# First FFN stage: shift and scale from ScalarE scalings and a VectorE tree, 1/rms applied ahead, a look-ahead of two chunks, four classical pairs

## The chip, the core and the metric

The kernel runs on one core of one Trainium2 chip, in one launch, for a batch of one sequence of 512 tokens, model width 1024, hidden width 2816. The metric is the device time of that launch in microseconds. Five engines work side by side, each through its own instructions in order: TensorE (PE in the profile; its weight loads are PEld), VectorE (DVE), ScalarE (ACT), GpSimd (POOL) and SyncE (SP), which issues most of the DMA transfers. POOL issues the others, those that accumulate into on-chip memory and the stores.

## The reference

One decoder layer with three sub-layers, each with a norm that is scaled and shifted by columns computed from the condition `c`:

```python
def modulate(x, w, shift, scale):
    return rms_norm(x, w) * (1 + scale[:, None, :]) + shift[:, None, :]

def swiglu(h, w13, w2):
    gu = jnp.einsum('bsd,df->bsf', h, w13)
    g, u = jnp.split(gu, 2, axis=-1)
    return jnp.einsum('bsf,fd->bsd', jax.nn.silu(g) * u, w2)

c_act = jax.nn.silu(c)
mod = (jnp.einsum('bd,dn->bn', c_act, w_ada[l]) + b_ada[l]).reshape(b, N_SUB, 3, D_MODEL)
h = modulate(x, norm_w[l, 0], mod[:, 0, 0], mod[:, 0, 1])
x = x + 0.5 * mod[:, 0, 2][:, None, :] * swiglu(h, ffn_w13[l, 0], ffn_w2[l, 0])
h = modulate(x, norm_w[l, 1], mod[:, 1, 0], mod[:, 1, 1])
x = x + mod[:, 1, 2][:, None, :] * hybrid_mixer(h, ...)
h = modulate(x, norm_w[l, 2], mod[:, 2, 0], mod[:, 2, 1])
x = x + 0.5 * mod[:, 2, 2][:, None, :] * swiglu(h, ffn_w13[l, 1], ffn_w2[l, 1])
```

`hybrid_mixer` is latent attention beside a short gated convolution. All is float32. The work at issue lies in the first sub-layer: `mod[:, 0, 0]` and `mod[:, 0, 1]` (shift and scale), the norm, `h`, and the first products with `ffn_w13`.

## The kernel before, in words

**Layout.** x lies transposed, features on the 128 partitions, in KD = 8 chunks of 128 features by T = 512 tokens (two tiles x_in of four chunks each). Each float32 product is done as three matmuls on split operands (`mm3`, lines 132 to 135): high by high, low activation by high weight, high by low weight. A split (`split_to`, line 110) is a cast to the high part on ACT (line 111) and a subtract on DVE (line 112). A matmul is 128x128 by 256 columns.

**Shift and scale.** For chunk j a block of 1 MB of `w_ada` (tile ada, loaded by `ada01_load`, line 146) holds, for each of eight parts k of the condition, 128 shift and 128 scale columns. `ada_first` (200 to 207) multiplies it with `c_act` by 16 matmuls that have one moving column each (line 206), into ps, and `ada_finish` adds the bias on DVE into the columns of the tile mod (lines 186 and 188).

**The norm.** `Norm.add` squares a chunk on ACT (261) and sums it over the features: in sub-layer 0 by matmuls with a column of ones on PE (266, four per chunk), elsewhere by adding chunks on DVE (273) and four matmuls at the end (280). `rstd` (275) makes the power -1/2 on POOL, `spread` (287) turns it into rb, 1/rms along the tokens in all partitions (a matmul into PSUM, line 295). `chunk` (298) makes h of one chunk: x times g times rb on DVE (309), plus shift with the cast to the high part on ACT (310), the low part on DVE (311), and x plus shift on ACT, kept for later sums (314).

**The first FFN.** The hidden width is 22 tiles of 128. The first stage walks over the eight chunks and multiplies each with weights wfh, wfl of the first two hidden tiles (tiles pf_0 to pf_3: a gate and an up half for each, 24 matmuls per chunk); for chunk k it first issues, in `first_chunk` (758), the load of ada for chunk k+2, `ada_first` of chunk k+1, and then `chunk` of k. The remaining tiles come in jobs that `run` (453) works off. `pair_job` (520) computes a gate and up pair by a Strassen-Winograd scheme: seven products of 12 matmuls, with sums of h (T, made by `sums`, 316) and sums of weights: four loads and one more on SP (529) into sa and sb, two accumulating transfers on POOL (530, 531), and DVE sums (540, 543). `down_job` (586) multiplies the results a with the down weights d. The first down phase follows hidden tile 5, and takes 288 matmuls.

**Who sets the order.** A framework puts the instructions of each engine in an order of its own, from the program's order and its own estimates; each engine then runs strictly in that order. Blocks of 1 MB (17 buffers) hold x, ada, h, T and the raw weights: a load into one waits until its former user is done. In the first stage all eight PSUM banks are in use. SP's loads take eight lanes in turn, each waiting for the earlier one on its lane.

**Two further places.** `rope_tables` (709) makes the tables for the mixer on DVE and ACT, with eight operations on POOL (746); it is called behind the first stage. The norm of the mixer is taken in two halves of the tokens; `next(n1.steps)` (780) issues the `rstd` of the second half, whose matmuls are line 280, ahead of the mixer's latent products (800).

## Time and profile before

| | us |
|---|---|
| time, median of 3 runs (1147.9 to 1148.43) | 1147.91 |
| the profiled execution, its own time | 1150.7 |
| its span, first to last instruction | 1148.9 |
| its mean granted TensorE clock | 0.975 of full |

The span is cut into 40 equal slices of 28.7 us; a digit gives the busy share in tenths, PEclk the clock that was granted.

```profile
PE   8999799999999998999999999999999999999998
DVE  1228776984589757776747667747998468734873
ACT  3125434553355425455433433335764255524540
POOL 0000212201220011211100000001200221022001
PEclk9958899999999999999999999999999999999999
```

The rows are read from left to right: the first stage of the first FFN lies in slices 2 to 4, the mixer begins near slice 16. In the groups that the prediction shows, a row gives line, engine, operation, output and inputs by name, shapes, count, busy time, mean duration in ns, and the idle time ahead with what ended it. In lists of single rows the first two numbers are start and duration in us.

### The profile page before, as it was taken

What the parts mean: (1) busy time and instruction counts of PE and PEld (TensorE: products, weight loads), DVE (VectorE), ACT (ScalarE), POOL (GpSimd) and SP (SyncE); (2) the same over time, 40 slices, a digit from 0 to 9 for tenths busy, and PEclk for the clock granted to TensorE, in tenths of its full rate; (3) what the DMA queues carried; (4) which work ended last, traced back from release to release, by engine and by line L of the source; (5) the groups of instructions that cost most, each with busy time, mean ns of one, the idle gap of its engine ahead of it and who ended that gap; (6) DMA issues with size and microseconds to landing.
All of it is one profiled execution on the core that took longest, in us unless ns stands there. A gap on an engine that the chain in (4) does not pass through costs nothing.

```text
span 1148.9 us, 20412 instructions
## 1 busy us (share of the span) xinstructions
PE 1113.3 (97%) x8126; PEld 1051.3 (92%) x8126; DVE 772.8 (67%) x1312; ACT 494.1 (43%) x823; POOL 141.5 (12%) x173
## 2 busy tenths in 40 slices
PE   8999799999999998999999999999999999999998
PEld 7999799999999998888887777879999999999997
DVE  1228776984589757776747667747998468734873
ACT  3125434553355425455433433335764255524540
POOL 0000212201220011211100000001200221022001
PEclk9958899999999999999999999999999999999999
DMA  9342688957994643321135466854875985568452
GB/s 364 95 119 80 205 262 253 243 186 197 223 267 123 227 144 101 101 70 56 61 113 187 135 236 220 272 167 112 209 205 178 260 229 148 175 142 186 114 189 97
DMA packets 83984, 199.68 MB, mean 174 GB/s; under 512 B 9777, under 2 KB 12721, under 8 KB 80817
## 3 DMA queue, kind: packets, MB, share of 16 engines
q1 hardware_dynamic: 67408, 164.82, 43.2%
q0 software_dynamic: 16480, 33.56, 15.1%
q8 instruction: 63, 1.03, 0.4%
q14 instruction: 33, 0.26, 0.1%
HBM read 180.52 MB, written 17.83 MB: 173 GB/s over the span
## 4 chain that ended last, share of the span: by engine, by line
PE 71%; DMA 9%; issue 9%; DVE 7%; POOL 2%; ACT 1%; SPq 0%; POOLq 0%; DVEq 0%; ACTq 0%
PE g L133 5%; PE g L135 5%; PE g L134 5%; PE d L134 5%; PE d L133 5%; PE d L135 5%; PE u L133 4%; PE u L134 4%; PE u L135 4%; PE ps L206 3%; DMA sa<-in_w13a_dram 3%; PE pf L133 2%; PE pf L134 2%; PE pf L135 2%; PE p_gate L133 1%
## 5 line engine op out<-in xcount | busy, mean ns | idle before, releaser
L134 PE MATMUL d<-a,d_h 128*128 128x256 f32 x616 | 172.1, 279 | 0.0
L133 PE MATMUL d<-a,d_h 128*128 128x256 f32 x616 | 171.8, 279 | 0.0
L135 PE MATMUL d<-a,d_l 128*128 128x256 f32 x616 | 171.6, 279 | 0.0
L133 PE MATMUL u<-T,w_h 128*128 128x256 f32 x480 | 135.3, 282 | 2.5 <-ACT s L560 2.5
L134 PE MATMUL u<-T,w_h 128*128 128x256 f32 x480 | 134.7, 281 | 0.3 <-DVE T L112 0.3
L135 PE MATMUL u<-T,w_l 128*128 128x256 f32 x480 | 134.6, 280 | 0.0
L111 ACT CAST w_h<-sa 128x1024 fp32r<-128x1024 f32 x80 | 83.7, 1049 | 86.9 <-issue 52.6
L112 DVE TENSOR_TENSOR w_l<-sa,w_h 128x1024 fp32r<-128x1024 f32 x80 | 97.8, 1224 | 30.6 <-ACT w_h L111 16.6
L134 PEld LDWEIGHTS d<-a,d_h 128*128 128x128 f32 x616 | 115.9, 188 | 0.4 <-DVE a L112 0.3
L135 PEld LDWEIGHTS d<-a,d_l 128*128 128x128 f32 x616 | 116.2, 189 | 0.0
L133 PEld LDWEIGHTS d<-a,d_h 128*128 128x128 f32 x616 | 116.0, 189 | 0.2 <-ACT a L111 0.2
L133 PE MATMUL g<-h,w_h 128*128 128x256 f32 x320 | 90.1, 282 | 6.3 <-ACT s L565 6.2
L133 PEld LDWEIGHTS u<-T,w_h 128*128 128x128 f32 x480 | 91.1, 190 | 3.4 <-ACT s L560 3.4
L135 PEld LDWEIGHTS u<-T,w_l 128*128 128x128 f32 x480 | 91.7, 191 | 0.0
L134 PEld LDWEIGHTS u<-T,w_h 128*128 128x128 f32 x480 | 90.8, 189 | 0.5 <-DVE T L112 0.5
L134 PE MATMUL g<-h,w_h 128*128 128x256 f32 x320 | 89.9, 281 | 0.0
L135 PE MATMUL g<-h,w_l 128*128 128x256 f32 x320 | 89.9, 281 | 0.0
L133 PEld LDWEIGHTS g<-h,w_h 128*128 128x128 f32 x320 | 60.8, 190 | 6.7 <-ACT s L565 6.4
L111 ACT CAST d_h<-wdd 128x1024 fp32r<-128x1024 f32 (+1 forms) x42 | 40.8, 977 | 58.3 <-issue 33.6
L135 PEld LDWEIGHTS g<-h,w_l 128*128 128x128 f32 x320 | 61.3, 191 | 0.0
L112 DVE TENSOR_TENSOR d_l<-wdd,d_h 128x1024 fp32r<-128x1024 f32 (+1 forms) x42 | 47.6, 1133 | 19.9 <-ACT d_h L111 13.4
L112 DVE TENSOR_TENSOR w_l<-sb,w_h 128x1024 fp32r<-128x1024 f32 x40 | 48.8, 1221 | 17.7 <-PE g L134 15.5
(347 smaller groups left out, 3144.5 us busy)
## 6 DMA issues: line engine op xcount, KB each, us to landing
ada<-in_ada_dram SPq DMA_DIRECT2D x24, 1024.0 KB, 6.9
sa<-in_w13a_dram SPq DMA_DIRECT2D x80, 256.0 KB, 5.1
sa<-in_w13b_dram SPq DMA_DIRECT2D x80, 256.0 KB, 5.2
wdd<-in_w_dram SPq DMA_DIRECT2D x32, 512.0 KB, 4.5
wr_ada<-in_ada_dram SPq DMA_DIRECT2D x24, 512.0 KB, 4.8
sa<-in_w13a_dram POOLq DMA_DIRECT2D x40, 256.0 KB, 6.5
sa<-in_w13b_dram POOLq DMA_DIRECT2D x40, 256.0 KB, 6.2
yd<-yd POOLq DMA_DIRECT2D x32, 256.0 KB, 5.5
```

Of the source, the lines that this page charges most:

```text
L111: nc.scalar.copy(out=hi, in_=src)
L112: nc.vector.tensor_tensor(out=lo, in0=src, in1=hi.bitcast(F32), op=ALU.subtract)
L133: nc.tensor.matmul(ps, a[0], b[0], start=first, stop=False, skip_group_check=parts)
L134: nc.tensor.matmul(ps, a[0], b[1], start=False, stop=False, skip_group_check=parts)
L135: nc.tensor.matmul(ps, a[1], b[0], start=False, stop=last, skip_group_check=parts)
L206: nc.tensor.matmul(ps[:, v : v + 1], w[:, k, v, :], c_act[:, k : k + 1], start=k == 0, stop=k == KD - 1)
```

## The change

Line numbers in this section are those of the changed kernel where a row is from it.

- **Shift and scale.** `ada_first` scales the eight parts of a block in place on ACT, each by its column of `c_act` (207), adds them as a tree on DVE in three steps (210), and sums over the partitions with two matmuls by a column of ones (213).
- **Squares of sub-layer 0** are added on DVE, as in the other sub-layers, with four matmuls at the end.
- **x times 1/rms** is done ahead on DVE, in place (790 and 795). `chunk` then makes the high part and the kept x by two ACT operations with g as scale and shift as bias (311, 312), and the low part by a subtract on DVE (313).
- **Look-ahead.** `first_chunk` of chunk k issues x times rb and `ada_first` for chunk k+2, and the loads of ada run one chunk further ahead; chunks 0 and 1 are prepared ahead of the loop.
- **Pairs.** The first stage of the first FFN makes three hidden tiles (36 matmuls per chunk, weight tiles of 768 columns) and `classic_job` makes a fourth by plain products: 96 matmuls where a Strassen-Winograd pair has 84.
- **Order around it.** The loads of the first two jobs are issued at the third-last and the last chunk; in the first FFN the splits of the first job and the evacuations come ahead of the sums T; `rope_tables` is called after the first store of the first down phase; `next(n1.steps)` comes behind the first latent products.

```diff
--- before.py
+++ after.py
@@ -37,7 +37,8 @@
 
 BUFS = {"ffn": {"slot": 5, "wide": 10, "sum": 4}, "mixer": {"slot": 11, "slot2": 4, "wr": 4, "wh": 4, "wl": 4}}
 WSUB = 512
-FIRST = (2, 2)
+FIRST = (3, 2)
+CLASSIC = (1, 0)
 HALF = T // 2
 
 PHASES = (((0, 6), (6, 14), (14, 22)), ((0, 8), (8, 16), (16, 22)))
@@ -199,11 +200,18 @@
 
     def ada_first(j):
 
-        w = w01[j].rearrange("p (k v c) -> p k v c", v=2, c=P)
+
+        w = w01[j]
+        for k in range(KD):
+            part = w[:, k * 2 * P : (k + 1) * 2 * P]
+            nc.scalar.activation(out=part, in_=part, func=AF.Copy, scale=c_act[:, k : k + 1])
+        for n in (4, 2, 1):
+            n *= 2 * P
+            nc.vector.tensor_tensor(out=w[:, :n], in0=w[:, :n], in1=w[:, n : 2 * n], op=ALU.add)
         ps = aux(f"ps01_{j}")
+        for v in range(2):
+            nc.tensor.matmul(ps[:, v : v + 1], w[:, v * P : (v + 1) * P], ones_c[:, 0:1], start=True, stop=True)
         for v in (1, 0):
-            for k in range(KD):
-                nc.tensor.matmul(ps[:, v : v + 1], w[:, k, v, :], c_act[:, k : k + 1], start=k == 0, stop=k == KD - 1)
             ada_finish(v, j, 1, ps[:, v : v + 1])
 
     ada_acc = {}
@@ -259,13 +267,7 @@
         def add(self, k, c0=0, n=T):
             sq = slot(f"sq{self.sub}_{k}_{c0}")
             nc.scalar.activation(out=sq[:, c0 : c0 + n], in_=self.x[k][:, c0 : c0 + n], func=AF.Square)
-            if self.sub == 0:
-                if k == 0:
-                    self.ss = aux("ps_ss0")
-                for b in range(NB):
-                    nc.tensor.matmul(self.ss[:, b : b + 1], sq[:, b * P : (b + 1) * P], ones_c[:, 0:1],
-                                     start=k == b == 0, stop=k == KD - 1, skip_group_check=True)
-            elif k == 0:
+            if k == 0:
                 self.acc = act.tile([P, T], F32, tag="nacc", name=f"nacc{self.sub}", bufs=1)
                 nc.vector.tensor_copy(out=self.acc, in_=sq)
             else:
@@ -275,8 +277,8 @@
         def rstd(self, b0, nb):
 
             s = f"{self.sub}_{b0}"
-            ps = self.ss if self.sub == 0 else aux(f"ps_ss{s}")
-            for b in range(nb if self.sub else 0):
+            ps = aux(f"ps_ss{s}")
+            for b in range(nb):
                 nc.tensor.matmul(ps[:, b : b + 1], self.acc[:, (b0 + b) * P : (b0 + b + 1) * P], ones_c[:, 0:1],
                                  start=True, stop=True)
             v = tmp.tile([P, NB], F32, tag="nv", name=f"nv{s}")
@@ -305,11 +307,16 @@
             hi, lo = cols(self.h[k], c0, n)
             g, sh = mod_col(3 * self.sub + 1, k), mod_col(3 * self.sub, k)
             x = self.x[k][:, c0 : c0 + n]
+            if self.sub == 0:
+                nc.scalar.activation(out=hi, in_=x, func=AF.Identity, scale=g, bias=sh)
+                nc.scalar.activation(out=x, in_=x, func=AF.Identity, scale=g, bias=sh)
+                nc.vector.tensor_tensor(out=lo, in0=x, in1=hi.bitcast(F32), op=ALU.subtract)
+                return
             t = slot(f"ht{self.sub}_{k}_{c0}")[:, :n] if self.sub == 1 else x
             nc.vector.scalar_tensor_tensor(out=t, in0=x, scalar=g, in1=rb[:, :n], op0=ALU.mult, op1=ALU.mult)
             nc.scalar.activation(out=hi, in_=t, func=AF.Identity, bias=sh)
             nc.vector.scalar_tensor_tensor(out=lo, in0=t, scalar=sh, in1=hi.bitcast(F32), op0=ALU.add, op1=ALU.subtract)
-            if self.sub != 1:
+            if self.sub == 2:
 
                 nc.scalar.activation(out=x, in_=x, func=AF.Identity, bias=sh)
 
@@ -583,6 +590,32 @@
 
             return load, prep, body
 
+        def classic_job(f):
+
+
+            def load(w):
+                w["raw"] = block(f"wc{i}_{f}")
+                for z in range(2):
+                    nc.sync.dma_start(out=w["raw"][:, z * D : (z + 1) * D], in_=(w13a, w13b)[i][f - first, z])
+
+            def prep(w):
+                for z in range(2):
+                    split_wide(w, w["raw"][:, z * D : (z + 1) * D], (z,), f"wc{i}_{f}_{z}", False)
+                    yield
+
+            def body(w):
+                banks = mm(f"g{i}_{f}"), aux(f"u{i}_{f}")
+                for z in range(2):
+                    for k in range(KD):
+                        for c in range(0, T, HALF):
+                            mm3(banks[z][:, c : c + HALF], cols(w[z], k * P, P), cols(norm.h[k], c, HALF),
+                                k == c == 0, k == KD - 1 and c > 0)
+                        if k % 4 == 3:
+                            yield
+                evac(f, *banks)
+
+            return load, prep, body
+
         def down_job(phase, ms, halves, keep=False):
 
 
@@ -646,6 +679,8 @@
                         else:
                             nc.gpsimd.dma_start(out=yd[m], in_=y)
                         ada_step(ADA[i][phase] // len(ms))
+                        if i == phase == m == 0:
+                            rope_tables()
                     else:
                         c, k = halves[0] * HALF, len(halves) * HALF
                         res.put(m, ps[:, c : c + k], c, k)
@@ -662,7 +697,7 @@
         pace_of = iter(pace)
         jobs = []
         for p, (f0, f1) in enumerate(PHASES[i]):
-            jobs += [pair_job(f) for f in range(max(f0, first), f1)]
+            jobs += [(classic_job if f < first + CLASSIC[i] else pair_job)(f) for f in range(max(f0, first), f1)]
             n_last = len(pace) if p == len(PHASES[i]) - 1 else 0
             both = [(m, m + 1) for m in range(0, KD, 2)]
             whole_chunks = both[: (KD - n_last) // 2]
@@ -671,14 +706,7 @@
 
         started = [{}, {}]
 
-        def sums(k):
-            norm.sums(k)
-            if k == 0:
-                jobs[0][0](started[0])
-            elif k == 2:
-                jobs[1][0](started[1])
-
-        ps = [(aux if t < (1, 2)[i] else mm)(f"pf{i}_{t}") for t in range(nt)]
+        ps = [(aux if t < (3, 2)[i] else mm)(f"pf{i}_{t}") for t in range(nt)]
         for c0, c1 in spans:
             for k in range(KD):
                 if len(wf) < KD:
@@ -688,19 +716,22 @@
                     for h0 in range(c0, c1, HALF):
                         mm3(ps[t][:, h0 : h0 + HALF], cols(wf[k], t * P, P), cols(norm.h[k], h0, HALF),
                             k == 0 and h0 == c0, k == KD - 1 and h0 == c1 - HALF)
-                if c1 - c0 == T and k >= KD // 2:
-                    sums(k - KD // 2)
-        if c1 - c0 < T:
-            for k in range(KD // 2):
-                sums(k)
-        first_prep = jobs[0][1](started[0])
-        drain(first_prep)
-        for f in range(first):
+                if c1 == T and k in (KD - 3, KD - 1):
+                    z = int(k == KD - 1)
+                    jobs[z][0](started[z])
+        if i == 0:
+            drain(jobs[0][1](started[0]))
+        for f in range(first if i == 0 else 0):
+            evac(f, ps[2 * f], ps[2 * f + 1])
+        for k in range(KD // 2):
+            norm.sums(k)
+        if i:
+            drain(jobs[0][1](started[0]))
+        for f in range(first if i else 0):
             evac(f, ps[2 * f], ps[2 * f + 1])
         if i == 0:
             nc.sync.dma_start(out=pk1, in_=pack1)
             nc.sync.dma_start(out=pos_i, in_=pos)
-            rope_tables()
         run(jobs, started)
 
 
@@ -752,15 +783,20 @@
     for k in range(KD):
         n0.add(k)
     n0.rstd(0, NB)
+    ada01_load()
     ada_first(0)
     rb0 = n0.spread(0, NB)
+    for k in range(2):
+        nc.vector.tensor_tensor(out=n0.x[k], in0=n0.x[k], in1=rb0, op=ALU.mult)
+    ada_first(1)
 
     def first_chunk(c0, k):
-        while len(w01) < min(k + 3, KD):
-            ada01_load()
-        if k + 1 < KD:
-            ada_first(k + 1)
-        n0.chunk(k, rb0)
+        if k + 2 < KD:
+            nc.vector.tensor_tensor(out=n0.x[k + 2], in0=n0.x[k + 2], in1=rb0, op=ALU.mult)
+            while len(w01) < min(k + 4, KD):
+                ada01_load()
+            ada_first(k + 2)
+        n0.chunk(k, None)
 
     x1d = dram.tile([KD, P, T], F32, name="x1d")
     x2d = dram.tile([KD, P, T], F32, name="x2d")
@@ -777,7 +813,6 @@
         hl = hl[:, : 2 * CPROJ], hl[:, 2 * CPROJ : 4 * CPROJ]
         split_to(*hl, raw[:, : 2 * CPROJ])
         wc += [cols(hl, i * CPROJ, CPROJ) for i in range(2)]
-    next(n1.steps)
     enter("mixer")
     kr_raw = act.tile([P, NB, DR], F32, name="kr_raw")
     cst = act.tile([P, NB, 4], F32, name="cst")
@@ -1045,6 +1080,7 @@
             next(under, None)
 
     drain(latent_products(0))
+    next(n1.steps)
     second = latent_products(1)
     next(second)
     drain(n1.steps)
```

PE, in the first stage, where chunk 1 is worked on. pf are the accumulators of the hidden tiles, h_1 the chunk's high and low part, ps the columns of a later chunk. Before:

```order
L206 MATMUL ps_2_260<-c_act,ada_2_204 128x1 x8
L133 MATMUL pf_0_192<-h_1_280,wfh_0_196 128x256
L134 MATMUL pf_0_192<-h_1_280,wfh_0_196 128x256
L135 MATMUL pf_0_192<-h_1_280,wfl_0_197 128x256
L206 MATMUL ps_2_260<-c_act,ada_2_204 128x1 x8
L133 MATMUL pf_0_192<-h_1_280,wfh_0_196 128x256
L134 MATMUL pf_0_192<-h_1_280,wfh_0_196 128x256
L135 MATMUL pf_0_192<-h_1_280,wfl_0_197 128x256
L133 MATMUL pf_1_193<-h_1_280,wfh_0_196 128x256
```

In the changed kernel, the same place:

```order
L134 MATMUL pf_0_191<-h_1_289,wfh_0_197 128x256
L134 MATMUL pf_1_192<-h_1_289,wfh_0_197 128x256
L134 MATMUL pf_2_193<-h_1_289,wfh_0_197 128x256
L134 MATMUL pf_3_194<-h_1_289,wfh_0_197 128x256
L134 MATMUL pf_4_195<-h_1_289,wfh_0_197 128x256
L134 MATMUL pf_5_196<-h_1_289,wfh_0_197 128x256
L213 MATMUL ps_3_283<-ones_c,ada_3_206 128x1 x2
L135 MATMUL pf_0_191<-h_1_289,wfh_0_197 128x256
L136 MATMUL pf_0_191<-h_1_289,wfl_0_198 128x256
```

Before, the eight and eight one-column matmuls of chunk 2 stand ahead of and within chunk 1's first products; now two matmuls of chunk 3 stand behind the first six products of chunk 1.

ACT, in the same stage from chunk 3 to chunk 4 (h_3 and then h_0 of the second half; x_in are the kept chunks, wfr and wfh the stage's weights, ada the blocks of shift and scale). Before:

```order
L310 ACTIVATE h_3_389<-x_in_74,mod 128x512
L111 CAST wfh_4_418<-wfr_4_420 128x512
L314 ACTIVATE x_in_74<-x_in_74,mod 128x512
L310 ACTIVATE h_0_226<-x_in_75,mod 128x512
L314 ACTIVATE x_in_75<-x_in_75,mod 128x512
L310 ACTIVATE h_1_280<-x_in_75,mod 128x512
```

In the changed kernel, the same place:

```order
L311 ACTIVATE h_3_419<-x_in_74,mod 128x512
L112 CAST wfh_4_459<-wfr_4_461 128x768
L312 ACTIVATE x_in_74<-x_in_74,mod 128x512
L207 ACTIVATE ada_6_400<-ada_6_400,c_act 128x256 x8
L311 ACTIVATE h_0_225<-x_in_75,mod 128x512
L112 CAST wfh_4_459<-wfr_5_524 128x768
L312 ACTIVATE x_in_75<-x_in_75,mod 128x512
```

Between the h of two chunks now stand eight scalings of a block two chunks ahead, beside the weight cast (now 768 wide, one per chunk) and the kept x.

POOL, from the last accumulating transfers ahead of the first down phase (sa are raw weights of a pair, rt the rope tables, yd the stored down results). Before:

```order
L530 DMA sa_4_726<-in_w13a_dram 128x512
L531 DMA sa_4_726<-in_w13a_dram 128x512
L746 TENSOR_TENSOR rt_qsin<-pk_86,rope_tmp 128x4x16 x2
L746 TENSOR_TENSOR rt_ksin<-pk_86,rope_tmp 128x4x16 x2
L746 TENSOR_TENSOR rt_qcos<-pk_86,rope_tmp 128x4x16 x2
L746 TENSOR_TENSOR rt_kcos<-pk_86,rope_tmp 128x4x16 x2
L530 DMA sa_5_853<-in_w13a_dram 128x512
L531 DMA sa_5_853<-in_w13a_dram 128x512
L647 DMA yd_191<-yd_0_0_0_0_1265 128x512
L647 DMA yd_191<-yd_0_0_0_1_1311 128x512
L530 DMA sa_6_1413<-in_w13a_dram 128x512
```

In the changed kernel, the same place:

```order
L537 DMA sa_4_676<-in_w13a_dram 128x512
L538 DMA sa_4_676<-in_w13a_dram 128x512
L537 DMA sa_5_744<-in_w13a_dram 128x512
L538 DMA sa_5_744<-in_w13a_dram 128x512
L680 DMA yd_190<-yd_0_0_0_0_1159 128x512
L777 TENSOR_TENSOR rt_qsin<-pk_86,rope_tmp 128x4x16 x2
L777 TENSOR_TENSOR rt_ksin<-pk_86,rope_tmp 128x4x16 x2
L777 TENSOR_TENSOR rt_qcos<-pk_86,rope_tmp 128x4x16 x2
L777 TENSOR_TENSOR rt_kcos<-pk_86,rope_tmp 128x4x16 x2
L680 DMA yd_190<-yd_0_0_0_1_1241 128x512
L537 DMA sa_6_1343<-in_w13a_dram 128x512
L538 DMA sa_6_1343<-in_w13a_dram 128x512
```

The rope operations stood between the transfers of pair 4 and those of pair 5; now they stand behind both and between the first two stores of the down phase, ahead of pair 6.

## The prediction, made before the result was known

> **What bounds the kernel now.** I read the page's totals first, then the groups of instructions and the waits of the opening, then TensorE (PE) row by row.
>
> ```profile
> span 1148.9 us, 20412 instructions
> PE 1113.3 (97%) x8126; PEld 1051.3 (92%) x8126; DVE 772.8 (67%) x1312; ACT 494.1 (43%) x823; POOL 141.5 (12%) x173
> ```
>
> PE is busy 97% of the span, so time can come only from fewer or faster matmuls, or from the few places where PE stands. The change touches the opening (up to the first down matmul) and one place in the mixer. Two views of the opening, groups on PE and waits (total, times, longest):
>
> ```profile
> L206 PE MATMUL ps<-c_act,ada 128*128 128x1 f32 x256 | 44.4, 303 | 0.2 <-DVE mod L186 0.2
> L133 PE MATMUL pf<-h,wfh 128*128 128x256 f32 x64 | 25.1, 416 | 1.0 <-ACT h L310 1.0
> L135 PE MATMUL pf<-h,wfl 128*128 128x256 f32 x64 | 23.1, 376 | 0.0
> DVE mod L186 <- PE ps L206: 47.6, 15, 5.6
> ACT h L310 <- DVE mod L186: 41.1, 5, 11.4
> ```
>
> The 256 matmuls with one column take 44 us of PE; VectorE (DVE) waits 48 us for them, ScalarE (ACT) 41 us for DVE. Only PE is a bottleneck there. Now single rows: start, duration.
>
> ```profile
> 28.02 1.01 PE L133 MATMUL pf<-h,wfh 128*128 128x256 f32 x3 [1.01 <-ACT h L310]
> 52.70 0.41 PE L134 MATMUL pf<-h,wfh 128*128 128x256 f32 x1
> 52.91 0.41 PE L135 MATMUL pf<-h,wfl 128*128 128x256 f32 x1
> 53.77 1.88 PE L206 MATMUL ps<-c_act,ada 128*128 128x1 f32 x16
> 55.72 0.28 PE L134 MATMUL pf<-h,wfh 128*128 128x256 f32 x1
> 55.83 0.28 PE L135 MATMUL pf<-h,wfl 128*128 128x256 f32 x1
> 153.08 0.28 PE L133 MATMUL d<-a,d_h 128*128 128x256 f32 x1
> ```
>
> A 128x256 matmul is issued 0.213 us after its neighbour at 52.70 and 0.113 us at 55.72: PE has a half and a full speed, which I read from these spacings. The first stage begins at 28.02, the first down matmul at 153.08: **125.1 us** that the change rearranges. Where they go:
>
> ```profile
> 28.00:106.50 78.50, 76.91 (x425) 75.88 (x425) 30.85 (x67) 19.58 (x28) 3.67 (x4) 0.78 0.29 84
> 132.83:139.08 6.25, 0.00 (x1) 0.01 (x1) 4.49 (x6) 3.70 (x6) 0.00 (x0) 0.74 0.70 255
> 143.56:153.24 9.68, 9.68 (x88) 9.68 (x87) 9.45 (x16) 4.39 (x7) 0.00 (x0) 1.00 0.65 231
> 188.06:197.74 9.68, 9.68 (x88) 9.68 (x87) 9.07 (x16) 5.02 (x7) 2.31 (x3) 1.00 0.79 264
> ```
>
> (Columns: stretch, length, busy time of PE, weight load, DVE, ACT, POOL, clock, DMA share, GB/s.) The first stage takes some 78 us for 192 wide matmuls worth 192 x 0.113 = 21.7 us at full speed. An undisturbed pair takes 9.68 us. In between PE stands 6.25 us, and the chain of waits says why:
>
> ```profile
> 121.64 1.99 POOL rt_qcos L746 x2
> 123.63 1.99 POOL rt_kcos L746 x2
> 125.62 0.53 POOL sa L530
> 126.16 7.39 DMA sa<-in_w13a_dram
> 139.08 0.58 PE g L133
> ```
>
> POOL's rope work delays the accumulating transfer of pair 4.
>
> **The change part by part.** I build the new time of the first down matmul.
>
> *Start.* Sums of squares leave PE: four matmuls in place of 32, after eight DVE operations behind the last input. Then rb follows at about 21 us as now, with the ACT scalings of ada_0 and ada_1 beside it. Estimated from the rows of the next fence: scalings done at 15.8 and 19.1, rb at 21.2, first scaled chunk at 23.2. The new `L313` of chunk 0 stands on DVE behind some 5 us of tree, weight split and x times rb, so the second product kind starts near 28. I take **28.0, as now**; bounds -2 to +4.
>
> *Eight chunks.* Prices:
>
> ```profile
> L310 ACT ACTIVATE h<-x_in,mod 128x512 fp32r<-128x512 f32 x8 | 5.8, 720 | 50.8 <-DVE mod L186 41.1 <-DVE x_in L309 9.7
> 438.57 1.30 ACT L310 ACTIVATE h<-ht,mod 128x256 fp32r<-128x256 f32 x3
> 110.81 0.37 ACT L560 COPY s<-u 128x256 f32<-128x256 f32 x1 [1.34 <-PE u L135]
> 111.08 0.60 ACT L565 COPY s<-g 128x512 f32<-128x512 f32 x1
> 146.34 1.56 ACT L111 CAST d_h<-wdd 128x768 fp32r<-128x768 f32 x2
> L112 DVE TENSOR_TENSOR T<-T,T 128x1024 fp32r<-128x1024 f32 x4 | 4.9, 1222 | 1.1 <-ACT T L111 1.1
> L112 DVE TENSOR_TENSOR wfl<-wfr,wfh 128x512 fp32r<-128x512 f32 x8 | 5.2, 686 | 0.0
> L323 DVE TENSOR_TENSOR T<-x_in,x_in 128x256 f32<-128x256 f32 x4 | 1.7, 418 | 0.0
> 146.10 0.95 DVE L112 TENSOR_TENSOR d_l<-wdd,d_h 128x768 fp32r<-128x768 f32 x1
> ```
>
> ACT, per chunk: 8 scalings of 128x256. The trace has no scaling by a column; the nearest row is the L310 of that size, three in 1.30 us, so a pitch of 0.40 if a lone one is 0.5, 0.43 at most: 3.2 us. Bounds: 0.27, the pitch of the plain copy of that size (110.81 to 111.08), and 0.5 if nothing overlaps: 2.2 to 4.0 us. Plus two 128x512 (2 x 0.72) and a 128x768 cast (0.78): **5.4 us**, 4.4 to 6.2. DVE: tree 1.22 + 0.69 + 0.42, x times rb 0.69, subtract 0.69, split 0.95: **4.7 us**, plus 0.5 of small ones. PE: 36 matmuls and two of one column (0.2 each, between the 1.88 / 16 of the row at 53.77 and the mean of 303 ns): 36 x 0.113 + 0.4 = **4.5 us** at full speed, 8.1 at half.
>
> ACT's 5.4 is above PE's 4.5, and still I say that PE sets the pace. ACT has the first chunk ready at 23.2; two scaled blocks stand ahead of the second (2 x 3.2 and 2 x 0.72: 31), and then 5.4 each gives 36.4, 41.8, 47.2 and 52.6 for chunks 2 to 5, after which no scalings are left. PE starts in earnest at 28.0, at half speed: its chunk 0 ends at about 36, chunk 1 (half of it slow) at 42.4, and it asks for chunks 2 to 5 at 42.4, 46.9, 51.4 and 55.9. ACT's lead is 6, 5, 4 and 3 us, of which the subtract behind it takes up to 2: just enough. Nothing else bends it, since the column matmuls of chunk k+2 lie inside chunk k, where the scaled block is ready. So chunks 2 to 5 end at 46.9, 51.4, 55.9 and 60.4, and the last two, with no column matmuls (4.1 each), at 64.5 and **68.6**.
>
> The slow start rests on how speed changes in the trace:
>
> ```profile
> 50.44:53.85 3.41, 3.41 (x19) 3.41 (x18) 0.75 (x1) 1.17 (x2) 0.00 (x0) 1.00 0.20 72
> 53.85:57.26 3.41, 3.41 (x32) 3.41 (x32) 1.07 (x3) 0.00 (x0) 0.00 (x0) 1.00 0.00 0
> 323.49:326.90 3.41, 1.48 (x13) 1.48 (x13) 2.70 (x5) 1.90 (x4) 0.00 (x0) 1.00 1.08 291
> 326.90:330.31 3.41, 3.41 (x19) 3.41 (x18) 1.45 (x3) 1.17 (x3) 1.73 (x2) 0.50 1.00 336
> ```
>
> A stretch of 3.41 us filled with wide matmuls (50.44) is followed by full speed (32 instructions in place of 19). One in which PE was busy for 1.48 of 3.41 us, with one gap of 1.93 us, is followed by half speed. So PE, dense from 28.0 on, should run at full speed some 5 to 8 us later; how small a gap keeps it there, no row here tells. The Trainium skill, "TensorE: Matmul & The Clock Gate", Part 1, has the same free-running 3413 ns window with two speeds, but would keep full speed through any gap under about 3 us. The trace differs: 1.93 us was enough. By the page the first rival below would cost 1.6 us less, since no gap of a chunk reaches 3 us; by the rows it keeps them.
>
> *Classical pair 3, pairs 4 and 5.* The first stage makes three pairs, so a pair of 84 matmuls moves into 12 more matmuls per chunk (in the 36 above); the fourth is 96 x 0.113 = 10.9 us, with 0.3 us for its bank (an activation and a product behind the last chunk; 0 to 1.3): 68.9 to 79.8. Then two pairs at 9.68: 99.2, and 1 us for small waits of the kind the groups show (0.2 to 1.0 ahead of some product): the first down matmul at **100.2**. DVE's list between 69 and 80 (three evacuations 3.6, four T splits 4.5, pair 4's weights and sums 5) is some 10 to 12 us long and pair 4 first needs only T_0 and one weight, so I add nothing; bound +3. Pair 4's load needs the block of ada_4, free when chunk 2 has run its column matmuls (near 44), so it lands by 53, needed at 80. Pair 5's load needs the block of the fourth pair's weights (split on ACT and DVE behind chunk 7's h, near 61), and a load and an accumulation of the length above (7.39) end near 72, needed at 89. Rope now lies on POOL behind these two and ahead of pair 6, which is needed after a down phase of 35 us: hidden; without that cover it is 8 us on POOL.
>
> Sum: 153.1 - 100.2 = **52.9 us**.
>
> *Mixer.*
>
> ```profile
> 442.50 0.61 PE L280 MATMUL ps_ss<-ones_c,nacc 128*128 128x1 f32 x4 [3.32 <-DVE nacc L273]
> 440.70 1.01 DVE L112 TENSOR_TENSOR wc<-wr_wc,wc 128x832 fp32r<-128x832 f32 x1
> ```
>
> PE waits 3.32 us for the last sum of squares; moved behind the first latent products, that wait can be filled, but these need the weight split that ends at 441.7: gain **0.9 us**, 0 to 3. FFN1's loads of its first two jobs come a chunk or two earlier into a busy PE: 0, bounds -1 to +1.
>
> Total 52.9 + 0.9 = 53.8. Profiled execution: 1150.7 (span 1148.9 and 1.8 around it) - 53.8 = 1096.9. It stands 2.8 over the median 1147.91, so against the median 1094.1; I forecast **1094**.
>
> **The rivals.** *ACT sets the pace.* With p for a scaling, chunk 5 is ready at 33.4 + 48 p; it is late from 53.9, p = 0.43. At p = 0.5 it is ready at 57.4 and PE starts it at 59.4 instead of 55.9: +3.5, and a stretch with such gaps may fall to half speed (+1.6): +5, **1099**. For it: 0.43 is near my 0.40. Against: the row of three. *Half speed throughout the first stage*, if gaps come in each stretch: chunks 2 to 7 cost 3.6 more each, 21.6, and the rest of chunk 1 about 2: +23, **1117**. Against: at half speed ACT is faster than PE, PE has no gaps, and dense stretches bring full speed. *A new wait ahead of pair 4 or 5*, like the 6.25 us now, with a cold stretch of 1.6 behind: +7, **1101**. For it: DVE is busy 9.45 of 9.68 in a pair already. *Slower:* the look-ahead fails, since tiles share a buffer or the in-order queue of ACT holds a scaled block behind h, and each chunk runs its chain alone: scalings 3.2, tree 2.3, column matmuls and mod 1.0, h 0.7, x 0.7, subtract 0.7, 36 matmuls 4.1 = 12.7 us; 28 + 8 x 12.7 = 129.6, and 30.6 for the fourth pair's 11.2 and two pairs at 9.7: 160.2 against 153.1, +7.1 less the mixer's 0.9: **1154**. It turns slower than before above (153.1 - 30.6 - 28) / 8 = 11.8 us per chunk. Against: the program issues x times rb and scaling for k+2 ahead of h of k. *The change doesn't do what it says*, the columns' matmuls staying on PE's path: excluded by the counts, 16 instead of 256.
>
> **How the numbers follow.** Forecast 0.57 (1087 to 1098), ACT's pace 0.20, a new wait 0.12, half speed 0.08, slower 0.02, within 0.2% (about what a measurement of this kernel can tell from no change) 0.01. Downward the bounds give -2 (start), -2 (mixer) and -3 (speed comes a stretch earlier): 1087. Upward the range takes in ACT's pace and the new wait with +4 of the start and +3 of DVE's list: 1108. Half speed and the slow case stay out, with a part of the forecast's own tails.
>
> **What would show it.** First down matmul near 100 in the new trace; about 16 column matmuls in 3 us; PE spacings of 0.113 from about 37 on; a pair still 9.68; PE's gaps between 37 and 100 under 3 us in sum; the 6.25 us gone; ACT's scalings at a pitch near 0.40. Wrong would be a PE that waits for ACT's h in every chunk, or a stop ahead of pair 4.

## The result and the profile after

The changed kernel takes 1094.13 us, the median of four executions (1089.48 to 1097.2); the kernel before, with one execution more than shown above, has the same median of 1147.91 (1134.99 to 1148.43). The ratio is 0.9554, 95% interval 0.9475 to 0.9632. The profiled execution took 1097.2, its span is 1095.4. In a later measurement with six executions of the changed kernel and eleven of the kernel before, the medians were 1093.33 and 1145.32, ratio 0.9584 (0.9535 to 0.9633). The ratios are formed from the fast executions alone (one of the eleven was a slow one), not from these medians. Forecast were 1094, with 1087 to 1108 as the range.

The page of the profile after, totals and two rows of slices (27.4 us each here):

```profile
span 1095.4 us, 19960 instructions
PE 1046.0 (95%) x7870; PEld 982.7 (90%) x7870; DVE 782.3 (71%) x1326; ACT 513.9 (47%) x877; POOL 135.7 (12%) x169
PE   2999989999999989999999989899999999999997
PEclk9999999999999989999999999899999999999999
```

PE's busy time fell by 67 us, the span by 53.5. The groups of the opening (to 97.2 us):

```profile
L135 PE MATMUL pf<-h,wfh 128*128 128x256 f32 x96 | 27.5, 298 | 1.3 <-DVE h L313 1.3
L213 PE MATMUL ps<-ones_c,ada 128*128 128x1 f32 x32 | 5.3, 268 | 8.8 <-DVE ada L210 8.8
```

The one-column matmuls went from 256 records and 44.4 us to 32 and 5.3. (Each such matmul of the program leaves two records: 16 per chunk were 32. The prediction's "16 instead of 256" sets matmuls against records; in records it is 32 instead of 256.) The mean of a pf matmul fell from between 376 and 416 ns, by line, to about 295 ns: most of the first stage now runs at full speed. The windows of the opening and of pairs 6 to 13, with the columns as before:

```profile
24.47:67.22 42.75, 40.33 (x314) 39.28 (x314) 38.27 (x79) 36.88 (x72) 3.69 (x4) 1.00 0.69 221
67.19:77.90 10.71, 10.71 (x95) 10.71 (x95) 10.57 (x13) 8.66 (x12) 0.00 (x0) 1.00 0.74 248
77.97:87.65 9.68, 9.68 (x88) 9.68 (x87) 9.00 (x14) 5.46 (x8) 0.00 (x0) 1.00 0.73 241
132.47:217.24 84.77, 80.79 (x674) 80.22 (x673) 72.13 (x107) 43.64 (x62) 9.23 (x11) 0.98 0.74 220
```

The first stage takes 42.75 us where it took 78.5, the fourth pair 10.7, a Strassen pair 9.68. The last row has something new in it: pairs 6 to 13 take 84.77 us, with 4 us in which PE stands. In the kernel before they took 78.15, without a stop:

```profile
188.06:266.21 78.15, 78.15 (x674) 77.98 (x673) 69.06 (x103) 43.77 (x62) 9.20 (x11) 1.00 0.77 229
```

Two single rows of the changed kernel, and the table of stages made from such rows:

```profile
97.23 0.28 PE L134 MATMUL d<-a,d_h 128*128 128x256 f32 x1
149.61 0.47 PE L134 MATMUL u<-T,w_h 128*128 128x256 f32 x1 [3.63 <-ACT s L567]
```

| stage, in the two profiled executions | before | after | difference |
|---|---|---|---|
| start to first down matmul | 153.08 | 97.23 | -55.85 |
| first down phase | 34.98 | 35.24 | +0.26 |
| pairs 6 to 13 | 78.15 | 84.77 | +6.62 |
| second down phase to the last down matmul of the first FFN | 172.69 | 172.15 | -0.54 |
| from there to the first p_xv matmul of the mixer | 16.18 | 16.68 | +0.50 |
| to the start of the second FFN | 337.96 | 342.51 | +4.55 |
| second FFN to the last matmul | 350.30 | 340.88 | -9.42 |

The opening gave more than the span shows. 6.6 us were given back in pairs 6 to 13, where a stop of 3.63 us was not there before. The last two rows, +4.55 and -9.42, lie in code that the change leaves alone, but for an order in the mixer. Over the fourteen profiles of this study, of whatever kernel, the first of these stretches lies between 336.4 and 345.9 us and the second between 339.8 and 352.3, so neither difference is shown to come from the change. The stop and the second FFN are taken up below.

### The profile page after: what moved, and what is told of

Same layout as the page of the kernel before. It is cut to its first block, busy times and chain, and to the rows that moved or that the text cites. A ratio compares the mean times of both kernels' runs of the same rounds, so it can differ in the third digit from the quotient of the medians.

```text
span 1095.4 us, 19960 instructions
## 1 busy us (share of the span) xinstructions
PE 1046.0 (95%) x7870; PEld 982.7 (90%) x7870; DVE 782.3 (71%) x1326; ACT 513.9 (47%) x877; POOL 135.7 (12%) x169
## 3 DMA queue, kind: packets, MB, share of 16 engines
q0 software_dynamic: 15904, 32.51, 15.3%
## 4 chain that ended last, share of the span: by engine, by line
PE 76%; DVE 10%; DMA 7%; issue 3%; ACT 1%; SPq 1%; POOL 1%; POOLq 0%; DVEq 0%; ACTq 0%
PE g L134 6%; PE g L135 6%; PE g L136 6%; PE d L135 6%; PE d L136 6%; PE d L134 6%; PE u L134 5%; PE u L135 5%; PE u L136 5%; DMA sa<-in_w13a_dram 2%; DMA wr_ada<-in_ada_dram 2%; DVE ada_acc L199 2%; PE pf L135 1%; PE pf L136 1%; PE pf L134 1%
## 5 line engine op out<-in xcount | busy, mean ns | idle before, releaser
L134 PE MATMUL u<-T,w_h 128*128 128x256 f32 x456 | 127.8, 280 | 4.0 <-ACT s L567 4.0
L135 PE MATMUL u<-T,w_h 128*128 128x256 f32 x456 | 127.3, 279 | 0.0
L136 PE MATMUL u<-T,w_l 128*128 128x256 f32 x456 | 127.2, 279 | 0.0
L112 ACT CAST w_h<-sa 128x1024 fp32r<-128x1024 f32 x76 | 79.8, 1050 | 81.7 <-issue 48.5
L113 DVE TENSOR_TENSOR w_l<-sa,w_h 128x1024 fp32r<-128x1024 f32 x76 | 92.5, 1220 | 20.5 <-ACT w_h L112 10.8
L134 PEld LDWEIGHTS u<-T,w_h 128*128 128x128 f32 x456 | 86.2, 189 | 4.9 <-ACT s L567 4.8
L136 PEld LDWEIGHTS u<-T,w_l 128*128 128x128 f32 x456 | 86.7, 190 | 0.0
L135 PEld LDWEIGHTS u<-T,w_h 128*128 128x128 f32 x456 | 86.1, 189 | 0.0
L134 PE MATMUL g<-h,w_h 128*128 128x256 f32 x304 | 84.6, 278 | 0.0
L135 PE MATMUL g<-h,w_h 128*128 128x256 f32 x304 | 84.4, 278 | 0.0
L136 PE MATMUL g<-h,w_l 128*128 128x256 f32 x304 | 84.4, 278 | 0.0
L547 DVE TENSOR_TENSOR sb<-sa 128x512 f32<-128x512 f32 x38 | 26.0, 684 | 53.7 <-DMA sa<-in_w13a_dram 32.6
L113 DVE TENSOR_TENSOR d_l<-wdd,d_h 128x1024 fp32r<-128x1024 f32 (+1 forms) x42 | 47.7, 1135 | 16.8 <-ACT d_h L112 11.2
L136 PEld LDWEIGHTS g<-h,w_l 128*128 128x128 f32 x304 | 57.4, 189 | 0.0
```

The costliest lines, as they stand in the source:

```text
L112: nc.scalar.copy(out=hi, in_=src)
L113: nc.vector.tensor_tensor(out=lo, in0=src, in1=hi.bitcast(F32), op=ALU.subtract)
L134: nc.tensor.matmul(ps, a[0], b[0], start=first, stop=False, skip_group_check=parts)
L135: nc.tensor.matmul(ps, a[0], b[1], start=False, stop=False, skip_group_check=parts)
L136: nc.tensor.matmul(ps, a[1], b[0], start=False, stop=last, skip_group_check=parts)
L547: nc.vector.tensor_tensor(out=b[:, 0], in0=a[:, 3], in1=a[:, 1], op=ALU.add)
```

## The experiments

Since a whole time moves by 5 to 19 us from one execution to the next, single executions are read by their stages: "first down" is the time of the first down matmul (97.23 in the changed kernel), and so on. Except where rounds are named, each is one profiled execution. All edits are to the changed kernel, but for `only_columns`.

**undo_columns**: the 16 one-column matmuls per chunk back on PE.

```diff
-            nc.scalar.activation(out=part, in_=part, func=AF.Copy, scale=c_act[:, k : k + 1])
...
+                nc.tensor.matmul(ps[:, v : v + 1], w[:, k, v, :], c_act[:, k : k + 1], start=k == 0, stop=k == KD - 1)
```

> The changed kernel with the 16 one-column matmuls per chunk back on TensorE, everything else kept (look-ahead of two, three first pairs, four classical). First down matmul now at 97.2 us. If only their own time counts (0.11 each at full speed), a chunk costs some 1.3 us more: first down matmul near 107. If they also hold the clock at half speed, a chunk costs 36 x 0.213 + 16 x 0.2 = 10.9 us: 28 + 8 x 10.9 less a few us, and 30 behind it: near 140.

First down at 127.14, 29.9 later; the first stage takes 67.0, and PE is busy in 66.86 of it. Two rows of column matmuls in it:

```profile
43.39 1.84 PE L208 MATMUL ps<-c_act,ada 128*128 128x1 f32 x16
45.53 1.90 PE L208 MATMUL ps<-c_act,ada 128*128 128x1 f32 x16
```

The granted clock changes only at steps of 3.41 us (or multiples). Here are stretches between such steps. In the first three rows only the wide matmuls, those of pf, are counted (start and end, length, busy time on PE, on PEld, on DVE and ACT, clock, DMA share, GB/s). The fourth is the whole row of the stretch behind the second, the fifth that of the stretch behind the third:

```profile
45.49:48.90 3.41, 1.81 (x15) 1.64 (x14) 0.00 (x0) 0.00 (x0) 1.00 0.12 24
52.32:55.73 3.41, 1.17 (x8) 1.02 (x9) 0.00 (x0) 0.00 (x0) 1.00 0.00 0
79.62:83.04 3.42, 1.75 (x12) 1.60 (x13) 0.00 (x0) 0.00 (x0) 1.00 0.00 0
55.73:59.15 3.42, 3.42 (x19) 3.42 (x18) 0.69 (x1) 3.00 (x4) 0.30 (x1) 0.50 0.64 178
83.04:86.45 3.41, 3.41 (x19) 3.41 (x18) 3.41 (x9) 2.57 (x3) 0.00 (x0) 0.50 0.02 5
```

Neither number came; the truth lies between them. The wide matmuls reach full speed at 42.0 us, but three times they fall back to half speed (granted clock 0.50) for one stretch, though PE never stands. Each time most of the stretch ahead went to column matmuls: 1.81 us of wide matmuls kept full speed, 1.75 and 1.17 did not. All fourteen profiles agree. Where matmuls of more than one column ran for 1.8 us or more of such a stretch at full speed, full speed followed; where they ran for 1.5 us or less, half speed followed; in between both occur. So column matmuls keep PE busy but do not keep it fast, and the first stage before, with 24 wide matmuls per chunk in place of 36, ran mostly at half speed.

The 29.9 us come, to within a microsecond, from three parts. A chunk has two groups of 16 records, at full speed some 3.4 us of PE, where I had counted one: the groups in the stage take 21.4 us more than the changed kernel's. The three slow stretches cost some 4.5 (16 matmuls each at 0.213 instead of 0.12), and pf starts 4.7 later.

**only_columns**: the kernel before with this one edit.

```diff
+            nc.scalar.activation(out=part, in_=part, func=AF.Copy, scale=c_act[:, k : k + 1])
...
+            nc.vector.tensor_tensor(out=w[:, :n], in0=w[:, :n], in1=w[:, n : 2 * n], op=ALU.add)
```

> The kernel before with this one edit (scalings on ScalarE, tree on VectorE, two one-column matmuls). If the one-column matmuls were most of the loss, ScalarE sets a pace of about 5.3 us per chunk: first stage 28 to 71, two Strassen pairs more than the changed kernel has and the old stop of 6.25: first down matmul near 116 instead of 153.1. If the look-ahead of two is what makes the scalings bearable, each chunk runs serially at about 11 us: near 150.

First down at 120.81, 4.8 later than the 116 of the first case: this edit alone gives 32.3 of the 55.85 us. The first stage, and what PE waited for in it (total, times, longest):

```profile
28.34:79.55 51.21, 38.65 (x231) 35.41 (x231) 44.91 (x88) 39.65 (x78) 4.52 (x5) 0.87 0.49 142
PE pf L133 <- ACT h L316: 8.6, 7, 2.9
```

PE stands 12.6 of 51 us: ScalarE's and VectorE's chain sets the pace here, though not serially. Of what makes up the other 23.5 us, the look-ahead and the sharing of the hidden tiles are tried below; the squares on VectorE, x times 1/rms ahead of time and the order of splits and evacuations were not tried by themselves.

**ahead_one**: look-ahead of one chunk.

```diff
-        if k + 2 < KD:
-            nc.vector.tensor_tensor(out=n0.x[k + 2], in0=n0.x[k + 2], in1=rb0, op=ALU.mult)
+        if k + 1 < KD:
+            nc.vector.tensor_tensor(out=n0.x[k + 1], in0=n0.x[k + 1], in1=rb0, op=ALU.mult)
...
-            ada_first(k + 2)
+            ada_first(k + 1)
```

> The changed kernel with a look-ahead of one chunk (x times 1/rms and scalings for k+1 ahead of h of k). If TensorE sets the pace and ScalarE's list only has to be ahead by about 2 us: first down matmul within 2 us of 97.2, perhaps earlier, since one block less stands ahead of chunk 1's h. If the second chunk of look-ahead is needed: TensorE waits in each chunk, 1.5 us or more each, first down matmul at 109 or later.

First down at 96.88, 0.35 earlier; pf begins at 22.43 instead of 24.47. With x times 1/rms and the scalings ahead of h, one chunk of look-ahead is enough; the second brings nothing here.

**slow_scaling**: four extra copies per block on ScalarE.

```diff
+            if k < 4:
+                nc.scalar.activation(out=part, in_=part, func=AF.Copy, scale=1.0)
```

> The changed kernel with four extra plain ScalarE copies of 128x256 per block, in place, beside the eight scalings (output unchanged). ScalarE's list grows by 1.6 us per block, chunk 5's h is ready near 64 instead of 51.6. By the prediction's bound (TensorE waits once a scaling costs over 0.43, here an effective 0.60): first down matmul some 10 to 13 us later, near 109. If ScalarE has more slack than that, or something else sets the pace: under 4 us later.

```profile
L209 ACT ACTIVATE ada<-ada 128x256 f32<-128x256 f32 x32 | 11.3, 402 | 0.0
64.47 0.49 PE L215 MATMUL ps<-ones_c,ada 128*128 128x1 f32 x3 [1.39 <-DVE ada L212]
```

First down at 109.08, 11.85 later, as the bound said. PE now waits 1.2 to 1.4 us in each of four chunks (the row shows the last) and more ahead of the first. ScalarE's list was short enough, as predicted. This is one point beyond the bound, at an effective 0.60; where between 0.40 and 0.60 the waits begin was not tried.

**two_pairs** and **no_classic**: the other ways to share the hidden tiles.

```diff
-FIRST = (3, 2)
-CLASSIC = (1, 0)
+FIRST = (2, 2)
+CLASSIC = (0, 0)
```

(`two_pairs`, which also puts the accumulators back into the banks that they had for two tiles; `no_classic` keeps FIRST at 3 and sets CLASSIC to 0.)

> The changed kernel with two hidden tiles in the first stage and four Strassen pairs behind it, as before the change (24 matmuls per chunk; 24 fewer in all). If matmul count decides: 2.7 us earlier, first down matmul near 94.5. If ScalarE's 5.35 us per chunk becomes the pace, TensorE stands about 2 us in each chunk and some of it at half speed: first stage ends near 60, four pairs of 9.7 follow: 98 to 104.

> The changed kernel with three hidden tiles in the first stage, but the fourth as a Strassen pair (12 matmuls fewer, no classical job). If matmul count decides: 1.4 us earlier, first down matmul near 95.8. If the fourth pair's plain products cover VectorE's T sums and splits (done at 76.4 in the changed kernel, first stage done at 67.2), TensorE waits for T behind the first stage: a stop of 3 us or more there, part of it at half speed, first down matmul at 101 to 106.

First down at 111.67 and 105.51: 14.4 and 8.3 later, with 24 and 12 matmuls less. The stretch behind the first stage in these two and in the changed kernel, for no_classic with what PE waited for up to the first down matmul:

```profile
62.30:75.00 12.70, 7.91 (x36) 6.54 (x34) 12.63 (x25) 6.33 (x8) 3.28 (x4) 0.69 1.03 256
```

```profile
67.47:79.00 11.53, 7.62 (x40) 6.04 (x39) 11.53 (x19) 7.11 (x9) 0.86 (x1) 0.84 0.82 230
PE u L135 <- DVE T L113: 2.6, 3, 0.9
```

```profile
67.22:78.75 11.53, 11.53 (x101) 11.53 (x102) 11.42 (x15) 9.43 (x12) 0.00 (x0) 1.00 0.76 259
```

VectorE is full in all three (12.63 of 12.70; 11.53; 11.42): it makes and splits the sums T, which a Strassen pair needs and a classical one does not. Without the classical pair PE gets two fifths of the matmuls done there (40 records in place of 101), with gaps and in part at half speed. The classical pair is the cover for T; for two_pairs I had looked for the wait in ScalarE and priced it at half its size.

**rope_slot** and **rope_old**: the stop at 146 us.

```diff
-        rope_tmp = block("rope_tmp")
+        rope_tmp = slot("rope_tmp")
```

(`rope_old` keeps the block and calls `rope_tables` behind the first stage again.) In the changed kernel the chain that leads to the stop has these rows, of GpSimd, of what SyncE's queue waited for (total, times, longest), of that queue, and of the chain of waits:

```profile
109.06 1.50 POOL L777 TENSOR_TENSOR rt_kcos<-pk,rope_tmp 128x64 f32<-128x64 f32 x2
SPq L227 <- POOL rt_kcos L777: 3.1, 1, 3.1
110.59 0.33 SPq L227 DMA_DIRECT2D ada<-in_ada_dram  x1
111.01 2.63 SPq L536 DMA_DIRECT2D sa<-in_w13a_dram  x4
114.28 12.51 DMA sa<-in_w13a_dram
```

The rope work ends at 110.56, and at 110.59 SyncE issues a load of ada that waited for the block of its scratch; the loads of pairs 7 and 8 follow at once.

> The changed kernel with the rope tables' scratch in a short 2 KB slot instead of one of the 17 blocks of 1 MB. The changed kernel has a new stop of 3.63 us at 145.98, ahead of pair 7's third product. If it comes from the block (SyncE's load of ada waits for GpSimd's rope work to free it, and the loads of pairs 7 and 8 stand behind that load): the stop is gone or under 0.5 us, and second down phase minus first down matmul falls from 120.0 to about 115. If it comes from GpSimd's 5 us themselves (stores and accumulating transfers late): it stays above 2.5 us.

> The changed kernel with the rope tables made behind the first stage, as before the change. By the prediction the rope work on GpSimd then stands ahead of nothing that is urgent, since the program now issues it behind the accumulations of pair 5: no stop of 6.25 us ahead of the first down matmul, which stays within 1.5 us of 97.2, and the stop at 146 is gone. If the old stop came from the rope work alone, a stop of 4 to 7 us returns ahead of pair 5 or the first down matmul.

```profile
132.48:209.21 76.73, 76.70 (x674) 76.34 (x673) 69.29 (x104) 43.80 (x62) 9.26 (x11) 1.00 0.78 234
```

```profile
134.10:211.06 76.96, 76.93 (x674) 76.57 (x673) 69.12 (x104) 43.79 (x62) 9.25 (x11) 1.00 0.78 233
```

Pairs 6 to 13 run without a stop in both, 76.73 and 76.96 us for 84.77; every kernel of this study that keeps the block in the down phase takes 83 to 86 there. In rope_slot GpSimd still does the rope work among the stores of the down phase, so its 5 us are not the cause; since two transfers of pair 6 also changed places with it there, the order on GpSimd is not excluded as a part. From first down to the second down phase it is 110.75 instead of 120.01, more than the 115 expected: 3.63 of the stop, half speed behind it, and a denser spacing (below). rope_old has no stop of 6.25 either: first down 99.45, 2.2 later than the changed kernel (1.5 were expected at most), with one gap of 0.83 us ahead of it. The move of `rope_tables` was not needed to lose the old stop, since rope then stands behind pair 5's transfers anyway.

**mixer_old**: the second half's 1/rms ahead of the latent products again.

```diff
+    next(n1.steps)
     enter("mixer")
...
-    next(n1.steps)
     second = latent_products(1)
```

> The changed kernel with the second half's 1/rms of the mixer's norm issued ahead of the latent products, as before. From the last down matmul of the first FFN to the first p_xv matmul it is 16.6 us in the changed kernel and 16.1 in the kernel before. If the prediction's gain of 0.9 is right and only the clock's window hides it: the wait ahead of the first latent products returns to about 3.3 us from 2.4, and the stretch as a whole comes out between 15.5 and 17.5. If the move costs something: the stretch falls to 15.5 or less with a wait under 2.4.

The first wait in mixer_old, and in the changed kernel with two rows of what follows:

```profile
392.92 0.61 PE L282 MATMUL ps_ss<-ones_c,nacc 128*128 128x1 f32 x4 [3.32 <-DVE nacc L275]
```

```profile
392.25 0.71 PE L135 MATMUL pc<-wc,h 128*128 128x416 f32 x1 [2.40 <-DVE wc L113]
398.47 0.55 PE L134 MATMUL pc<-wc,h 128*128 128x416 f32 x1
399.44 0.35 PE L134 MATMUL pc<-wc,h 128*128 128x416 f32 x1
```

The wait is 3.32 against 2.40: 0.92 as predicted. The stretch to p_xv is 16.10 in mixer_old, 16.18 in the kernel before, and 15.2 to 15.3 in seven of the single executions with the move (undo_columns, ahead_one, two_pairs, rope_slot, rope_old, slow_scaling, no_classic). In the changed kernel's profile it is 16.68, since there half speed lasts to 399 (0.55 rows, then 0.35); in another execution of it, 13.6. But the stretch ends too early to price the move. From the last down matmul to the last p_xv matmul it is 111.65 to 111.74 us in the three profiles without the move (before, only_columns, mixer_old) and 111.47 to 111.70 in those seven: less than 0.3 of the 0.9 is left, and what takes the rest was not looked for.

**Timed together, five rounds**: the changed kernel, the scratch in a slot, and the slot with a look-ahead of one.

> The changed kernel itself again, as the yardstick of this call: 1089 to 1097 us.

> The changed kernel with the rope scratch in a short slot. If the stop at 146 (3.63 us and some 1.6 at half speed behind it) is all that it removes: about 5 us under the changed kernel of this call on the median, both spread by some 8 us from one execution to the next.

> The rope scratch in a short slot and a look-ahead of one chunk. The look-ahead was worth 0.4 us in one look: within 2 us of the kernel with the short slot alone.

| kernel | median of 6 | lowest, highest | ratio to before, 95% |
|---|---|---|---|
| changed | 1093.33 | 1089.99, 1096.59 | 0.9584 (0.9535 to 0.9633) |
| rope_slot_timed | 1087.41 | 1082.59, 1091.01 | 0.9534 (0.9486 to 0.9581) |
| rope_slot_ahead_one | 1085.02 | 1084.21, 1089.38 | 0.9515 (0.9466 to 0.9563) |

The slot brings 5.9 us on the medians, about the stop and what hangs on it; the two together lie 8.3 under the changed kernel, and 2.4 under the slot alone where at most 2 were expected. The intervals of all three overlap, so only the order of the medians is shown.

## Why the prediction was right, step by step

- **Start.** Predicted 28.0 for the second kind of product. It begins at 26.79, 1.2 earlier. pf itself starts at 24.47, behind column matmuls of chunk 1 that wait 3.3 us for VectorE's tree (of the 8.8 in the L213 row; 4.4 belong to chunk 0, ahead of rb).
- **ScalarE's list.** Predicted: a scaling at 0.40, 5.4 us per chunk, h ready at 31, 36.4, 41.8, 47.2, 52.6. ScalarE's rows in the changed kernel:

```profile
29.39 0.80 ACT L311 ACTIVATE h<-x_in,mod 128x512 fp32r<-128x512 f32 x1
31.54 3.29 ACT L207 ACTIVATE ada<-ada,c_act 128x256 f32<-128x256 f32 x8
34.74 0.80 ACT L311 ACTIVATE h<-x_in,mod 128x512 fp32r<-128x512 f32 x1
36.89 3.29 ACT L207 ACTIVATE ada<-ada,c_act 128x256 f32<-128x256 f32 x8
```

  Eight scalings take 3.2 from 31.54 to 34.74, 0.40 each; h comes every 5.35 us, the second ready at 30.2. slow_scaling, beyond the limit, is late by about what was worked out from it.
- **PE's pace.** Predicted 4.5 per chunk at full speed from about 37, end 68.6. A chunk takes 4.76 (0.12 between matmuls, not 0.113), but full speed comes near 31; the end is 67.2. Two gaps of 0.55 us follow and from 37 us on none, so PE sets the pace as said. That dense work would bring full speed was too simple: in undo_columns PE is as dense and falls back. Here 36 wide matmuls stand beside two of one column.
- **Fourth pair and pairs 4 and 5.** 11.2 with its bank and twice 9.68 predicted, 10.8, 9.68 and 9.58 measured; the 1 us for small waits did not come. First down 97.23 for 100.2: the saving of 52.9 became 55.85. Why the classical pair costs nothing was not in the prediction. I counted its matmuls and found VectorE's list short enough; no_classic shows that the pair itself is what makes it so.
- **Rope "hidden".** This step failed. I looked at GpSimd's time and the 35 us ahead of pair 6, and not at the block that the scratch holds and at SyncE, whose queue waits for it with two pairs' loads behind. The rival of a new wait had the price (7 us) but the wrong place, ahead of pair 4 or 5 instead of within pair 7.
- **Mixer.** 0.9 predicted, 0.92 at the wait, about 0.9 up to the first p_xv matmul in most kernels, but under 0.3 up to the last. The prediction stopped at the wait. The profiled execution lost the 0.9 to half speed before that.
- **The sum.** 53.8 predicted and 53.5 in the span agree in part by luck: the opening gave 2.95 more than forecast, pairs 6 to 13 took back 6.6 that the prediction had put at nothing, and the rest comes from stages whose length moves by itself. Rows of them:

```profile
900.00:950.00 50.00, 50.00 (x428) 50.00 (x427) 31.41 (x43) 20.71 (x29) 12.00 (x16) 1.00 0.86 236
```

```profile
900.00:950.00 50.00, 50.00 (x443) 50.00 (x443) 42.28 (x60) 29.48 (x42) 5.13 (x6) 1.00 0.61 168
```

```profile
900.00:950.00 50.00, 50.00 (x427) 50.00 (x426) 40.53 (x58) 28.49 (x41) 3.45 (x4) 1.00 0.54 160
```

  These are the kernel before, the changed kernel and rope_old, 50 us in the second FFN each, PE busy throughout. The first and the third run 427 or 428 matmuls in it, the second 443.
- **Page and trace.** The prediction set the clock rule of the Trainium skill, "TensorE: Matmul & The Clock Gate", Part 1, against a gap of 1.93 us that brought half speed. After the change the first stage has only gaps of 0.55 us once it is at full speed, and keeps it; both readings agree with that. undo_columns does not agree with a rule of gaps alone: PE has no gap from 42 us to the end of its first stage and still falls to half speed three times. What fits all the profiles is how much of a stretch of 3.41 us the wide matmuls fill.

## What to carry to other kernels

Work that leaves the bottleneck engine for idle ones is worth its time on the bottleneck as long as the new engine's list per step, plus its lead, stays ahead; that limit can be worked out from rows of similar instructions, and here the times at which h was ready came within about a microsecond. Matmuls of one column cost more than their own time: in a stretch that they fill for the most part PE loses its full speed, so taking them off PE also makes the wide ones faster. When a job is moved under cover, look at the buffers it holds and at what stands behind the next user of each in an in-order queue, not only at its own engine. A product that costs more matmuls can be the cheaper one, if it needs less preparation from an engine that is late at that place.

## What the runs showed that I had not expected

PE runs dense 128x256 matmuls at full speed with two spacings: about 0.113 us (443 in 50 us) and 0.118 us (427), each for up to some 300 us at a stretch, with the granted clock given as 1.00 for both. A third, 0.120, shows in the first stage of the second FFN in every profile. The same second FFN takes 339.8 to 340.9 us in six profiles (two of the changed kernel, rope_slot, mixer_old, slow_scaling, no_classic) and 350.3 to 350.7 in five (before, undo_columns, only_columns, ahead_one, rope_old); the other three lie at 342.0, 343.4 and 352.3, the first two with both spacings within the FFN. The switches looked at come at small interruptions of the stream, of 0.1 to 0.2 us. What selects the spacing was not found. It may in part be the chip: four kernels that were run on one chip (undo_columns, only_columns, ahead_one, two_pairs) all have the wider spacing in the second FFN, but on another chip both occur. The spacing is worth up to 10 us of the spread of 5 to 19 us between executions of one kernel; that the phase at which half speed starts and ends makes up the rest is not shown. This is why the experiments were read by stages.
